# A half-swap of a matrix by memory-to-memory transfers: one walk over the rows replaced by eight

## The chip, the cores and the metric

The kernel runs on one core of one Trainium2 chip. Its time is the device time of the program in microseconds. It was run twice before the change: 822.33 us and 824.99 us, median 823.66 us.

## The reference

The input `x` is a matrix of 8192 x 8192 float32 numbers, 268.44 MB.

```python
def reference(x: np.ndarray) -> np.ndarray:
    return np.fft.ifftshift(x)
```

On an even-sized matrix this swaps the halves of both axes: output row `r` is input row `r + 4096` (modulo 8192), and in each row the left 4096 columns and the right 4096 columns change places. No number is changed. A row is 32 KiB long and half a row is 16 KiB, so everything the kernel does is to move 16384 runs of 16 KiB each from one place in the device memory to another.

## The kernel before, in words

There is no arithmetic and nothing is staged on chip. Two instruction streams, SyncE (SP, `nc.sync`) and ScalarE (ACT, `nc.scalar`), issue transfers that go straight from `x` to `out`, both of them in device memory. The core has 16 DMA engines, and the transfers of both queues run on the same 16.

`copy` (lines 26 to 32) issues one transfer: 256 rows of one half, 4 MiB. Its access pattern has three levels (line 28): 16 rows that lie next to each other, then 16 steps of `step * C` elements, then the 4096 elements of half a row. With `step = ENGINES = 16`, the outermost level counts neighbouring rows and the middle one jumps 16 rows ahead. The outermost level is the one that can be dealt out to the 16 engines. An engine that has index `k` of it moves rows `k`, `k + 16`, `k + 32` and so on, so that at one time the 16 engines are at 16 neighbouring rows, 32 KiB apart. The source address is that of row `row + 4096` and of the opposite half.

The loop (lines 36 to 39) takes 1024 rows at a time, which is four blocks of 256. For each block SP gets the left half of the output (`h = 0`), and ACT the right half (`h = hc`) of the block two further on, modulo four, so 512 rows away. Over the whole kernel SP writes the left half of `out` and ACT the right half, with 32 transfers each. The order of work is written out by hand; nothing but the two queues and the semaphores at which each transfer reports decides what runs when. The framework gives the transfers eight semaphores in turn, four to a queue, so that the fifth transfer of a queue is issued when the first one of that queue has landed.

Of the kernel before, what the change touches and what calls it, by code (L numbers as in the profile page):

```python
# [1 line left out]

# [4 lines left out]


ENGINES = 16


@with_exitstack
def kernel(
    ctx: ExitStack,
    tc: tile.TileContext,
    x: bass.AP,
    out: bass.AP,
):
    nc = tc.nc
    R, C = x.shape  # L20
    hr = R // 2
    hc = C // 2
    per = 16
    rows = ENGINES * per

    def copy(queue, row, h, step):

        dims = [[C, ENGINES], [step * C, per], [1, hc]]
        queue.dma_start(
            out=bass.AP(out.tensor, out.offset + row * C + h, dims),  # L30
            in_=bass.AP(x.tensor, x.offset + (row + hr) % R * C + hc - h, dims),
        )

    for first in range(0, R, 4 * rows):
        for n in range(4):
            copy(nc.sync, first + n * rows, 0, ENGINES)
            copy(nc.scalar, first + (n + 2) % 4 * rows, hc, ENGINES)


# [1 line left out]
_INS = ['x']  # L43
_OUTS = [((8192, 8192), 'float32')]


def kernel(**inputs):
    import numpy as _np
    import concourse.bacc as _bacc
    import concourse.tile as _tile  # L50
    from concourse import mybir as _mybir
    from concourse.bass_utils import run_bass_kernel_spmd as _run

    nc = _bacc.Bacc("TRN2", target_bir_lowering=False, num_devices=1)  # L54
    arrays, args = {}, []
    for name in _INS:
        a = _np.ascontiguousarray(inputs[name])
        if a.dtype.kind in "iu":
            a = a.astype(_np.int64)
        arrays[f"in_{name}_dram"] = a  # L60
        args.append(nc.dram_tensor(f"in_{name}_dram", a.shape, _mybir.dt.from_np(a.dtype), kind="ExternalInput").ap())
    for i, (shape, dtype) in enumerate(_OUTS):
        dt = _mybir.dt.from_np(_np.dtype(dtype))
        args.append(nc.dram_tensor(f"out_{i}_dram", shape, dt, kind="ExternalOutput").ap())
    with _tile.TileContext(nc) as tc:
        kernel(tc, *args)
    r = _run(nc, [arrays], core_ids=[0])
    got = tuple(r.results[0][f"out_{i}_dram"] for i in range(len(_OUTS)))
    return got[0]
```

## Time and profile before

| | |
|---|---|
| median of the two timed runs | 823.66 us |
| span of the profiled execution (first to last instruction) | 812.4 us |
| its own whole time | not given apart from the span |
| bytes read, bytes written | 268.44 MB, 268.44 MB |
| transfers | 32 on SP, 32 on ACT, 4096 KB each |
| duration of one issue (median) | 571 ns on SP, 578 ns on ACT |
| from issue to landing (median) | 101.0 us |

The profile of this kernel has hardly any compute in it: four small constants that GpSimd sets at the start. What there is to read are the rows on the DMA engines. "DMA" is the mean busy share of the 16 engines, "GB/s" is what they moved in one direction (every byte is read once and written once, so the memory sees twice that). A packet is one run of 16 KiB, or the short write by which an engine reports a finished transfer. Times in a table of windows count from the start of the span, and a packet is counted whole in the window in which it starts, so that the share of a short window can exceed 1.

### The profile page before, as it was taken

The numbers are of one execution on the slowest core, as the hardware profiler recorded it, in microseconds if no ns is written. First come the engines' busy times: TensorE is split into PE (matmuls) and PEld (weight loads), VectorE is DVE, ScalarE is ACT, GpSimd is POOL, SyncE is SP. The second block draws the span as 40 slices with busy tenths as digits, with TensorE's granted clock in tenths as the row PEclk, the third lists the DMA queues.
The fourth block names the chain that finished last, engine by engine and source line by source line (L and its number), as shares of the span: only waits on it lengthen the run. The fifth ranks groups of instructions, "written<-read, shape, count | busy, mean of one in ns | idle before, by whom it ended". The sixth has DMA issues, their size and how long they took to land. (4 is left out here: it accounts for less than half of the span.)

```text
span 812.4 us, 109 instructions
## 1 busy us (share of the span) xinstructions
POOL 0.2 (0%) x4
## 2 busy tenths in 40 slices
POOL 0000000000000000000000000000000000000000
DMA  9999999999999999999999999999999999999998
GB/s 307 331 331 336 335 331 331 335 325 337 334 332 336 331 333 332 334 339 332 332 334 331 329 331 334 332 328 333 330 334 335 334 328 333 332 331 330 338 331 280
DMA packets 17408, 268.44 MB, mean 330 GB/s; under 512 B 1024, under 2 KB 1024, under 8 KB 1024
## 3 DMA queue, kind: packets, MB, share of 16 engines
q1 hardware_dynamic: 8704, 134.22, 49.7%
q10 hardware_dynamic: 8704, 134.22, 49.5%
HBM read 268.44 MB, written 268.44 MB: 661 GB/s over the span
## 5 line engine op out<-in xcount | busy, mean ns | idle before, releaser
L54 POOL MEMSET const-bfloat16-1.0<- 128x1 bf16 x1 | 0.1, 101 | 0.0
L54 POOL MEMSET const-uint8-127<- 128x1 uint8 x1 | 0.1, 101 | 0.0
L54 POOL MEMSET const-float32-0.0<- 128x1 f32 x1 | 0.1, 98 | 0.2 <-issue 0.2
L54 POOL MEMSET const-float32-1.0<- 128x1 f32 x1 | 0.1, 98 | 0.0
## 6 DMA issues: line engine op xcount, KB each, us to landing
out_dram<-in_x_dram SPq DMA_DIRECT2D x32, 4096.0 KB, 101.0
out_dram<-in_x_dram ACTq DMA_DIRECT2D x32, 4096.0 KB, 101.0
```

The costliest lines, as they stand in the source:

```text
L54: nc = _bacc.Bacc("TRN2", target_bir_lowering=False, num_devices=1)
```

## The change

The loop is replaced by eight walks of 1024 rows each, one after the other, that cover the 8192 rows. All of them make `copy` transfers of another form, and each differs from the others in the order of the halves, in the distance between the rows of the two queues, or in both.

```diff
-    per = 16
-    rows = ENGINES * per
+    block = 256
+    part = 4 * block
-    def copy(queue, row, h, step):
-
-        dims = [[C, ENGINES], [step * C, per], [1, hc]]
+    def copy(queue, row, order, rows=block):
+        h = order[0] * hc
+        dst = out.offset + row * C + h
+        src = x.offset + (row + hr) % R * C + hc - h
+        to, of = [[C, rows]], [[C, rows]]
+        if len(order) == 2:
+            step = (order[1] - order[0]) * hc
+            to, of = to + [[step, 2]], of + [[-step, 2]]
         queue.dma_start(
-            out=bass.AP(out.tensor, out.offset + row * C + h, dims),
-            in_=bass.AP(x.tensor, x.offset + (row + hr) % R * C + hc - h, dims),
+            out=bass.AP(out.tensor, dst, to + [[1, hc]]),
+            in_=bass.AP(x.tensor, src, of + [[1, hc]]),
         )
+    def walk(first, sync, scalar):
+        for a, b in zip(sync, scalar):
+            copy(nc.sync, first + a[0] * block, a[1])
+            copy(nc.scalar, first + b[0] * block, b[1])
+    def whole(blocks, order):
+        return [(b, order) for b in blocks]
+    def halves(blocks, order):
+        return [(b, (h,)) for b in blocks for h in order]
+    def near(first):
+        for row in range(first, first + part // 2, ENGINES):
+            copy(nc.sync, row, (1, 0), ENGINES)
+            copy(nc.scalar, row + part // 2, (1, 0), ENGINES)
-    for first in range(0, R, 4 * rows):
-        for n in range(4):
-            copy(nc.sync, first + n * rows, 0, ENGINES)
-            copy(nc.scalar, first + (n + 2) % 4 * rows, hc, ENGINES)
+    left = [(b, (0,)) for b in (0, 1, 2, 3)]
+    right = [(b, (1,)) for b in (2, 3, 0, 1)]
+    for n, (sync, scalar) in enumerate((
+        (left, right),
+        (whole((0, 2), (1, 0)), whole((1, 3), (1, 0))),
+        (whole((0, 1), (1, 0)), whole((2, 3), (1, 0))),
+        (whole((0, 2), (0, 1)), whole((1, 3), (0, 1))),
+        (halves((0, 2), (0, 1)), halves((1, 3), (0, 1))),
+        (halves((0, 1), (0, 1)), halves((2, 3), (0, 1))),
+        (whole((0, 2), (1, 0)), whole((1, 3), (0, 1))),
+        (None, None),
+    )):
+        if sync is None:
+            near(n * part)
+        else:
+            walk(n * part, sync, scalar)
```

In words, with the walks numbered 0 to 7:

- Walk 0 has the same blocks, halves and queues as before (SP left halves, ACT right halves 512 rows away). Only the pattern is another: its outermost level counts 256 rows.
- Walks 1, 2, 3 and 6 move whole rows, 256 at a time (8 MiB), both halves of a row in turn: the pattern is 256 rows, 2 halves, 4096 elements. Walk 1 takes the right half of the output first and has the queues 256 rows apart; walk 2 does the same 512 rows apart; walk 3 is walk 1 with the left half first; in walk 6 SP takes the right half first and ACT the left half first, 256 rows apart.
- Walks 4 and 5 move one half of 256 rows in one transfer and then the other half in the next, left first on both queues; the queues are 256 rows apart in walk 4 and 512 in walk 5.
- Walk 7 (`near`) moves whole rows, right half first, but in transfers of 16 rows (512 KiB), 32 of them per queue, with the queues 512 rows apart.

Where the outermost level has 256 rows and an engine takes 16 successive ones, the 16 engines are 16 rows or 512 KiB apart at one time. In walk 7, as before the change, they are at neighbouring rows. The built program has per queue, in this order: 4 transfers of one half; 4 of whole rows; 2 of whole rows; 8 of one half; 2 of whole rows; 32 small ones: 52 in place of 32. The runs stay 16 KiB long, and there are 16384 of them as before.

## The prediction

> **What bounds the kernel now.** I read the page from the top. Compute is nothing, so the first rows that matter are those on the DMA engines, in forty slices of 20.3 us, and the totals by queue.
>
> ```profile
> span 812.4 us, 109 instructions
> DMA  9999999999999999999999999999999999999998
> GB/s 307 331 331 336 335 331 331 335 325 337 334 332 336 331 333 332 334 339 332 332 334 331 329 331 334 332 328 333 330 334 335 334 328 333 332 331 330 338 331 280
> DMA packets 17408, 268.44 MB, mean 330 GB/s; under 512 B 1024, under 2 KB 1024, under 8 KB 1024
> q1 hardware_dynamic: 8704, 134.22, 49.7%
> q10 hardware_dynamic: 8704, 134.22, 49.5%
> HBM read 268.44 MB, written 268.44 MB: 661 GB/s over the span
> ```
>
> The 16 DMA engines carry packets for 99.2% of the span (49.7% + 49.5%), half of it for each queue, and the rate lies between 325 and 339 GB/s in every slice but the first and the last. So the time is packets times the time of one: 17408 packets less 1024 short reports are 16384 runs of 16 KiB, 1024 to an engine, and 0.992 x 812.4 / 1024 is 787 ns each. Only a change of that 787 ns can move the time much.
>
> Next come the issues of line 29, and what SP waits for.
>
> ```profile
> L29 SPq DMA_DIRECT2D out_dram<-in_x_dram x32: 571/571/652, 0.7 to 708.6; - x32
> L29 ACTq DMA_DIRECT2D out_dram<-in_x_dram x32: 578/578/881, 0.7 to 713.5; - x32
> DMA to landing us min/median/max: 25.6/101.0/103.4
> ```
>
> ```profile
> SPq L29 <- DMA out_dram<-in_x_dram: 689.4, 28, 25.3
> ```
>
> An issue takes 0.57 us; 28 of SP's 32 wait for a transfer to land (24.6 us each), and a transfer lands 101.0 us after its issue, four periods of 25.3. Each queue is four transfers ahead. The issue side is idle 97% of the time.
>
> Last, is 787 ns a fixed cost? The table of windows shows the beginning and the end (columns: window, length, GpSimd busy, clock, DMA share, GB/s).
>
> ```profile
> 2.20:3.20 1.00, 0.00 (x0) 1.00 0.97 262
> 3.20:5.20 2.00, 0.00 (x0) 1.00 1.09 426
> 5.20:7.20 2.00, 0.00 (x0) 1.00 0.90 328
> 7.20:9.20 2.00, 0.00 (x0) 1.00 1.08 377
> 9.20:13.20 4.00, 0.00 (x0) 1.00 1.00 319
> ...
> 808.00:810.00 2.00, 0.00 (x0) 1.00 0.54 180
> 810.00:812.40 2.40, 0.00 (x0) 1.00 0.02 7
> ```
>
> The first packet starts about 2.2 us into the span. From 2.2 to 9.2 us the mean is (262 + 2 x 426 + 2 x 328 + 2 x 377) / 7 = 361 GB/s, and from then on it is 319 to 339. In the first 3 us only SP's queue has packets, and the 16 engines began together; the trace's packets of that time last 611 to 690 ns after a first set of about 1000, and 611 ns is also about the shortest of the whole run. So an engine can carry a packet in 611 ns, and in the steady state it takes 787: the memory behind all 16 holds them back. The last packets end within some 2 us of each other, so the engines keep step to the end.
>
> **The sum to start from.** 268.44 MB at the steady 332 GB/s is 808.6 us. The other 15.1 us of the 823.66 us median are 3.8 us of the span (its start, the uneven end) and 11.3 us around the span; the change touches none of them. One walk of 1024 rows is 33.55 MB, 101.1 us.
>
> **The change part by part.**
>
> *Bytes and packets.* The runs stay 16 KiB and 16384 in number: 0 us. Transfers rise from 64 to 104, so reports from 1024 to 1664; in the trace a report occupies its engine for 9 ns, so 640 / 16 x 9 ns = 0.4 us, added.
>
> *Issues, walks 0 to 6.* 20 issues per queue of 4 or 8 MiB. One of 512 rows of runs may take as long as two of 571 ns, 1.1 us. What hides it is the four transfers already queued, 101 us or more: 0 us; with no cover it would be 20 x 1.1 = 22 us. At a joint of two walks nothing waits, since the queues run on.
>
> *Issues, walk 7.* 32 issues of 512 KiB on each queue, one per 3.2 us if the rate holds (33.55 MB / 332 / 32). The issue takes 0.57 us of it. The four-deep lead shrinks to 4 x 2 x 0.524 MB = 4.2 MB, or 12.6 us of work. A slot comes back when the slowest engine has reported: about 2 us of unevenness (the end rows), 0.57 us of issue, 1.5 us from issue to first packet (0.7 to 2.2 us), some 4 us in all. Hidden: 0 us. Without the lead, each of the 32 rounds would cost up to 4 us, 128 us; I take 0, since 12.6 is three times 4.
>
> *The order of addresses, seven walks.* Before, 16 engines are at 16 neighbouring rows. In walks 0 to 6 they are 512 KiB apart (if an engine takes 16 successive rows of the 256), and in walks 1, 2, 3, 6 and 7 an engine does both halves of a row in turn. No row of this trace has such a spacing. The nearest ones are the rates that the same traffic takes by chance in short stretches, here in forty slices of 5 us:
>
> ```profile
> GB/s 331 324 338 334 351 315 315 338 344 331 341 321 351 334 324 344 288 357 331 347 324 321 354 315 347 315 334 360 334 328 341 328 341 338 341 321 331 338 324 344
> ```
>
> Five of forty are at 315 or less and five at 351 or more; I take these as the ends. Seven walks are 234.9 MB: 707.5 us at 332, 745.7 at 315 (+38), 669.2 at 351 (-38). I take 332, so 0. The reason is that the 20 us slices don't vary though queue, blocks and addresses do: each engine gets its sixteenth of a shared rate, and the same rate holds in the slices where one queue happens to have most of the packets as where they are even. That is how a limit on the sum of reads and writes looks, 661 GB/s, and the sum is not changed.
>
> Here the Trainium skill has a rule against the change. "DMA: Bandwidth & Descriptors", in "Latency and other measured facts", gives copies of 16 KiB pieces between memory tensors less rate at large power-of-two row pitches: 207 GB/s at 512 KiB against 214 unhampered, 164 at 2 MiB. By it the seven walks would take 214 / 207 x 707.5, 24 us more, an estimate of 848 us in all. No trace of this case has that pitch between engines yet.
>
> *Walk 7's addresses* are near ones, as now: 0 us; in turn or not, the same ends would be -5 and +5 us.
>
> Sum: 823.7 + 0.4 = 824 us.
>
> **The rivals.**
>
> *Slower: the engines collide.* Sixteen streams that stand 512 KiB apart and move in step hit the same parts of the memory at once more often than sixteen neighbouring rows do. For it: the engines do keep step, and the packets already lose 787 - 611 = 176 ns to something shared. Against it: with two queues an engine is rarely at the same point of its row as the next. At 315 GB/s in seven walks the time is 862 us. It decides from a rate of 324 in the seven walks, which is 725.0 us, 17 us more. If pairs of engines serialised outright, it could go far beyond; 288 GB/s, the lowest slice, would give 815.6 for the seven walks, 932 us. This is also where the Trainium skill's pitch rule ends.
>
> *Faster: the order matters and neighbouring halves help.* [...] For it: 361 GB/s in the first 7 us shows that the memory can give more to a more orderly pattern. Against it: that lasted 7 us of 809. At 361 in the five walks in turn (167.8 MB), these take 464.8 in place of 505.4 us, 783 us in all. It decides from 344 GB/s in these five, 17.6 us less. The Trainium skill's "HBM Reference", "Specifications (TRN2)", states about 716 GB/s for the memory of a pair of cores; the sum of 661 is 92% of it, and at 716 this kernel would take an estimated 750 + 15 = 765 us, so it leaves little room below.
>
> *The change doesn't do what it says.* If the 16 engines are dealt the rows of a 256-row transfer one by one, walk 0 is the kernel before, and only the order of halves changes elsewhere. Nothing in the trace says how rows are dealt. The time would be 824, so I count it with the forecast.
>
> *Walk 7 runs dry.* If a slot came back in 16 us and not 4, walk 7 would take 32 x 4 = 128 us in place of 101, 851 us in all. For it: only 512 KiB per transfer. Against it: the 4 us above.
>
> **How the numbers follow.** Forecast, no change of rate (or walks that cancel): 0.45, 824 us, own range 808 to 840. Engines collide: 0.31, around 862. Walk 7 dry: 0.04, 851. Neighbouring halves help: 0.20, around 783. A measurement of this kernel can tell some 2% from no change. Chances: faster 0.20, same 0.45, slower 0.35. The range of 8 in 10 leaves out the lower half of the fast case and the far end of the slow one: 788 to 875 us.
>
> **What would show it.** The eight walks come one after the other, so windows of about 101 us of the new profile price each by its GB/s: 325 to 339 in all eight would bear the forecast out. Below 324 in walks 0 to 6 with about 332 in walk 7 is the collision, and walk 0 alone is its clean test, since it differs from the kernel before only in the spacing. Above 344 in walks 1, 2, 3, 6 and 7 and not in 0, 4, 5 is the gain from neighbouring halves. A DMA share well below 1 in walk 7 is a queue run dry. What would make the forecast wrong is that the 787 ns depend on which addresses are in flight together, and not only on their sum.

## The result, and the profile after

The changed kernel takes 846.22 us (846.17 and 846.28), the kernel before 823.66 us: 1.029 times as long, 95% interval 1.022 to 1.035. That is slower, inside the range of 788 to 875 us, but not the likeliest case of the forecast, which was 824 us.

The page of the kernel after: the span, the rates in forty slices of 21.1 us, and the totals.

```profile
span 844.4 us, 149 instructions
DMA  9999999999999999999999999999999999999998
GB/s 301 331 322 317 331 308 315 303 317 303 310 319 307 313 311 310 315 311 309 314 326 331 323 335 326 332 328 330 331 326 310 313 316 314 304 321 329 331 328 294
HBM read 268.44 MB, written 268.44 MB: 636 GB/s over the span
```

The engines carry packets all the time, as before. The row that was flat (325 to 339) now has steps: four slices of 317 to 331 after the start, fifteen near 311, ten near 328, five near 311 again, and 321 to 331 at the end. Windows laid inside the eight walks give one number to each (columns: window, length, GpSimd busy, clock, DMA share, GB/s).

```profile
2.00:102.00 100.00, 0.00 (x0) 1.00 1.00 327
104.00:210.00 106.00, 0.00 (x0) 1.00 1.00 309
212.00:318.00 106.00, 0.00 (x0) 1.00 1.00 311
321.00:425.00 104.00, 0.00 (x0) 1.00 1.00 312
428.00:527.00 99.00, 0.00 (x0) 1.00 1.00 330
530.00:628.00 98.00, 0.00 (x0) 1.00 1.00 330
631.00:736.00 105.00, 0.00 (x0) 1.00 1.00 311
739.00:838.00 99.00, 0.00 (x0) 1.00 1.00 326
```

The DMA share is 1.00 in every walk, so no walk starves; the packets themselves take longer. Four walks are slow, 1, 2, 3 and 6, and these are the four that move both halves of a row in turn with the engines 16 rows apart. The three with halves apart (0, 4, 5) are not slow, though they were written for the same spacing (E1 below asks whether they have it), and neither is walk 7, in turn at neighbouring rows. Which half comes first (1 against 3), whether the queues are 256 or 512 rows apart (1 against 2) and whether they have like or opposite halves (1 against 6) makes 2 to 3 GB/s.

Four walks of 33.55 MB at 311 in place of the 329 that E1 below has on the same stretch of runs are 134.2 / 0.311 - 134.2 / 0.329 = 23.6 us; the measured difference is 22.6.

The waits of SP and the landing of the small transfers answer to the rows of issue shown before:

```profile
SPq L39 <- DMA out_dram<-in_x_dram: 607.6, 48, 53.6
```

```profile
out_dram<-in_x_dram SPq DMA_DIRECT2D x32, 512.0 KB, 12.8
```

48 of 52 issues wait for a landing, so SP is still four transfers ahead throughout, and a small transfer lands 12.8 us after its issue, four periods of 3.2.

### The profile page after: what moved, and what is told of

Its sections match the earlier page's. It is cut to its first block, busy times and chain, and to the rows that moved or that the text cites. A ratio compares the mean times of both kernels' runs of the same rounds, so it can differ in the third digit from the quotient of the medians.

```text
span 844.4 us, 149 instructions
## 1 busy us (share of the span) xinstructions
POOL 0.2 (0%) x4
## 6 DMA issues: line engine op xcount, KB each, us to landing
out_dram<-in_x_dram SPq DMA_DIRECT2D x32, 512.0 KB, 12.8
out_dram<-in_x_dram ACTq DMA_DIRECT2D x32, 512.0 KB, 12.8
```

## The experiments

Two notes for the numbers. The kernel before took 822.3 us beside E1 to E8 (run on chips 5 and 1) and 813.6 us beside E9 to E12 (chips 0 and 14), so rates of E9 to E12 are some 1% above those of the others and ratios are taken within a group. And most kernels here are surveys like the changed kernel itself: eight walks of 1024 rows, each read from a window of its own.

The first theory, A: the loss needs far engines and halves in turn together, because the runs in flight then lie at few different places of the memory, and collide there. Rivals: B, the large three-level transfer of whole rows is slow as a form; C, the spacing alone costs; D, halves in turn cost by themselves.

**E1, walk 0 in all eight places.**

```diff
-    for n, (sync, scalar) in enumerate((
-        ...
+    for n in range(8):
+        walk(n * part, left, right)
```

> All eight walks as walk 0: halves apart, queues in opposite halves, engines 512 KiB apart. Against the kernel before it changes the spacing of the engines alone. Theory A (the loss needs both, far engines and halves in turn, because then the runs in flight lie at few different places within the 512 KiB that an engine walks): 327 to 331 GB/s in every walk, the profiled span within 1.5% of that of the kernel before. Rival C (far spacing alone costs): walk 0 of the changed kernel had 327 GB/s where the kernel before had 334, so 2% slower in every walk.

Measured: 821.93 us against 822.27, ratio 0.9997 (0.9971 to 1.0023). Two of its walks:

```profile
412.00:508.00 96.00, 0.00 (x0) 1.00 1.00 331
514.00:610.00 96.00, 0.00 (x0) 1.00 1.00 326
```

All eight have 326 to 331, so this form of transfer costs nothing. What looked like 327 against 334 was the difference between two groups of runs.

That would end C if the engines of these walks really stood 512 KiB apart, which is not shown. In the trace, the issue of such a transfer is recorded as `dst_num_elem=[256,1]`, the inner count first, so with a count of 1 in the outer place. Every other form here has 16 or more in it: the kernel before `[16,16]`, walk 1 `[2,256]`, walk 3 `[1,512]`. If the engines are dealt the 256 rows one by one, they stand at neighbouring rows, as in the kernel before, and walk 0 has no new spacing. The times of the packets speak for that. Take a queue's packets in order of start, in sets of sixteen. In the kernel before, sets 0 to 3 and 8 to 11 of each 256 rows (rows 0 to 63 of each 128) took 825 ns a packet and the other sets 748. Averaged over walks and queues, the two groups of sets differ by 71 ns in walk 0 of the changed kernel and by 82 ns in walks 4 and 5 (there the other sets are the slow ones), but only by 21 ns in walks 1, 2, 3 and 6. E1 has 49 ns.

**E2, walk 1 in all eight places.**

```diff
+    for n in range(8):
+        walk(n * part, whole((0, 2), (1, 0)), whole((1, 3), (1, 0)))
```

> All eight walks as walk 1: whole rows in turn, right half first, queues 256 rows apart, 8 MiB transfers, engines 512 KiB apart. If the loss belongs to that form and not to the place of the walk in the kernel or in memory, every eighth has 309 to 312 GB/s and the time is 865 to 875 us, 2 to 3% above the changed kernel. If it came from the joints between unlike walks, it would be near 824 us.

Measured: 862.00 us, ratio 1.050 (1.045 to 1.054), 312 to 316 GB/s in every walk, about 3 us under what was expected. Walk 1:

```profile
112.00:214.00 102.00, 0.00 (x0) 1.00 1.00 312
```

The loss belongs to the form of the walk, not to its place in the kernel or to the joints.

**E3, form or place.** All in turn or nearly; transfers of 16 rows, one per engine, have the same small size as walk 7's.

```diff
+    def small_far(first, off=0):
+        for b in (0, 2):
+            for j in range(ENGINES):
+                r = first + b * block
+                copy(nc.sync, r + j, [("r", 16, ENGINES), ("h", -1, 2)], 1)
+                copy(nc.scalar, r + block + (j + off) % 16, [("r", 16, ENGINES), ("h", -1, 2)], 1)
```

> Eight walks of 1024 rows, queues 256 rows apart unless said. 0: in turn, 256-row transfers, as walk 1. 1: the same rows in the same order, but in transfers of 16 rows, one per engine, 512 KiB apart. 2: in turn, 16 neighbouring rows, as walk 7. 3, 4, 5, 7: halves change after every 2, 4, 8, 16 rows of an engine. 6: as 1, with ACT half a run (8 rows) away within each engine's 16 rows. Theory A (few places within the 512 KiB in flight at once): 0 and 1 near 311 GB/s, 2 near 326, 3 to 7 rising from 311 to 330 with the number of rows, and 6 above 1, about 325, since the queues then lie at different places. Rival B (the large three-level transfer of whole rows is what is slow): 0 near 311, 1 and 6 near 326 as 2 is, and 3, 4, 5, 7 all near 330. Rival D (both halves of a row one after the other by one engine cost by themselves, wherever the others are): 0, 1, 6 near 311, 3 to 7 at 330 at once.

| walk | GB/s |
|---|---|
| 0, in turn, 256 rows per transfer | 314 |
| 1, in turn, 16 rows per transfer, engines 16 rows apart | 310 |
| 2, in turn, 16 rows per transfer, neighbouring rows | 328 |
| 3, 4, 5, halves change after 2, 4, 8 rows | 314, 314, 311 |
| 6, as 1, ACT 8 rows off | 323 |
| 7, halves change after 16 rows (recorded as `[256,1]`, as in E1) | 329 |

Walk 1 is slow in transfers of 512 KiB, as slow as walk 0 in transfers of 8 MiB: B falls. (Walks 1 and 2 differ in the stride of one level and in the distance of the queues, 256 and 512 rows; E4 has both strides at 512 rows and the same difference.) Walk 6 shows that the place of one queue against the other counts. D fails on walks 3 to 5, and A's own rise over them did not come either: there is a jump between 8 and 16 rows. It falls where the recorded form changes, from `[8,16]`, which names the 16 places of the engines 16 rows apart, to `[256,1]`.

**E4, the spacing in turn.**

```diff
+    def turn(first, n):
+        for r in range(first, first + part // 2, 16 * n):
+            both(r, r + part // 2, [("r", 1, 16 * n), ("h", -1, 2)], 1)
```

> All walks but the last are in turn, queues 512 rows apart; the engines stand 1, 2, 4, 8, 16, 32 rows apart in walks 0 to 5 (transfers of 0.5 to 16 MiB), and 17 and then 15 rows apart in walk 6; walk 7 is halves apart at 16 rows. Theory A (few places within a power-of-two stretch in flight at once): 326 GB/s at 1, falling with the distance to 311 at 16 and as low or lower at 32; 17 and 15 bring it back to 325 to 331, since successive engines then stand at different places; walk 7 at 330. Rival B (the large transfer of whole rows): 1 and 2 near 326, the rest near 311, and 17 and 15 near 311 as well. Rival D (in turn by itself): all but the first near 311.

The walks at 8, 16 and 32 rows, the one at 17 and 15 rows, and the one with halves apart:

```profile
309.00:406.00 97.00, 0.00 (x0) 1.00 1.00 330
411.00:513.00 102.00, 0.00 (x0) 1.00 1.00 310
520.00:645.00 125.00, 0.00 (x0) 1.00 1.00 252
652.00:754.00 102.00, 0.00 (x0) 1.00 1.00 307
762.00:852.00 90.00, 0.00 (x0) 1.00 1.00 327
```

At 1, 2, 4 and 8 rows it is 328 to 330; the fall sets in between 8 and 16 rows (256 and 512 KiB), and 32 rows cost almost a quarter of the rate. An even fall from 1 on, as A had it, did not come. B and D, which had the rest near 311, fail at 4 and 8 rows. The odd spacing did not help, which is a miss of theory A as it stood. In these walks the rate follows the rows per transfer, so here each engine does take a run of successive rows; dealt one by one, all six would be the same.

**E5, one part undone: 8 rows in place of 16 in walks 1, 2, 3 and 6.**

```diff
-        (whole((0, 2), (1, 0)), whole((1, 3), (1, 0))),
-        ...
+    def eight(first, a, b, order):
+        for n in range(4):
+            copy(nc.sync, first + a[n] * part // 8, order[0], part // 8)
+            copy(nc.scalar, first + b[n] * part // 8, order[1], part // 8)
```

> The changed kernel with one edit: in walks 1, 2, 3 and 6 the transfers have 128 rows in place of 256, so that the engines stand 8 rows (256 KiB) apart and not 16; halves, their order and the distance of the queues stay. Theory A (the engines' spacing in turn is what costs): those four walks go from 309 to 312 up to 330 GB/s, and the time from 846 down to 820 to 824 us. Rival D (halves in turn cost by themselves): still about 845 us.

Measured: 823.73 us, ratio to the kernel before 1.002 (0.9997 to 1.004). Walks 1 and 2 are now

```profile
106.00:204.00 98.00, 0.00 (x0) 1.00 1.00 326
208.00:306.00 98.00, 0.00 (x0) 1.00 1.00 329
```

Halving the transfers of those four walks, and with them the distance between engines, brings the ratio from 1.029 to 1.002, with halves still in turn, in the same order, on the same queues. The smaller size by itself is not the reason: in E3, transfers of 512 KiB with the engines 16 rows apart are as slow as those of 8 MiB.

**E6, how far apart the two queues are within a run.** E3's `small_far` with eight offsets of ACT.

```diff
+    for n, off in enumerate((0, 1, 2, 4, 6, 8, 10, 12)):
+        turn(n * part, off)
```

> All walks in turn, engines 16 rows apart, 16 rows per transfer, queues 256 rows apart plus an offset: when SP's engines are at row j of their runs of 16, ACT's are at row j + 0, 1, 2, 4, 6, 8, 10, 12 (modulo 16) in walks 0 to 7. Theory A2 (what counts is whether the runs in flight lie in unlike 256 KiB groups of 8 rows): the two queues are in unlike groups for offset/8 of the time up to 8 and (16 - offset)/8 beyond; from 311 GB/s at 0 to 323 at 8 that gives 311, 312.5, 314, 317, 320, 323, 320, 317. Rival A1 (any unlike row will do, as it spreads them over all places): 311 at 0 and some 320 or more at once from 2 on. Rival E (the offset does nothing; 323 was chance): 311 in all.

```profile
2.00:107.00 105.00, 0.00 (x0) 1.00 1.00 309
110.00:214.00 104.00, 0.00 (x0) 1.00 1.00 310
219.00:321.00 102.00, 0.00 (x0) 1.00 1.00 312
326.00:427.00 101.00, 0.00 (x0) 1.00 1.00 318
432.00:530.00 98.00, 0.00 (x0) 1.00 1.00 323
536.00:633.00 97.00, 0.00 (x0) 1.00 1.00 327
639.00:737.00 98.00, 0.00 (x0) 1.00 1.00 324
743.00:840.00 97.00, 0.00 (x0) 1.00 1.00 319
```

In the reports of this run the transfers of the two queues land on average 0.3 us apart, a tenth of the time of a row, so the offset is the distance. The rate climbs evenly to 8 rows and comes back as evenly: 4 and 12 give 318 and 319, 6 and 10 give 323 and 324. That is the shape of A2, with a rise of 18 GB/s where 12 was expected: with an offset of d rows out of 16, the queues are in unlike 256 KiB groups for d / 8 of the time up to 8, and for (16 - d) / 8 beyond. From 309 to 327 nearly the whole loss is undone by moving ACT a quarter of a MiB. A1, any unlike row, and E, chance, fall.

**E7, halves apart: spacing, and queues that run even.**

```diff
+                copy(nc.sync, a + j, [("r", 16, ENGINES), ("r", 1, 2)], 0)
+                copy(nc.scalar, b + (j + off) % 16, [("r", 16, ENGINES), ("r", 1, 2)], 1)
```

> Halves apart, SP left and ACT right halves, queues 512 rows apart as in walk 0 (0 rows in walk 4). Walks 0 to 4: engines 4, 8, 16, 32, 64 rows apart. Walks 5 to 7: 16 rows apart, in transfers of 2 rows per engine, so that the queues run even, with ACT 0, 4 and 8 rows away within each run of 16. Theory A: 330 at 4, 8, 16, and then falling, below 311 at 32 and below 253 at 64, as fewer places are left; walk 5 falls to about 311, since large transfers were saved only by ACT being some 3 rows behind, and walk 7 is back at 323 to 330. Rival D (only halves in turn cost): 327 to 330 in all eight.

The walk at 64 rows in large transfers, and the three in transfers of 2 rows:

```profile
413.00:511.00 98.00, 0.00 (x0) 1.00 0.99 328
516.00:616.00 100.00, 0.00 (x0) 1.00 1.00 312
622.00:720.00 98.00, 0.00 (x0) 1.00 1.00 326
725.00:822.00 97.00, 0.00 (x0) 1.00 1.00 322
```

At 4, 8, 16, 32 and 64 rows large transfers of halves apart keep 326 to 329: the expected fall at 32 and 64 did not come. All five are recorded with an outer count of 1, so by the rival of E1 none of them has the spacing that it was written for. Walks 5 to 7 name it in a level of its own (`[2,16]`), and walk 5 shows that halves apart can lose as much as halves in turn. So D falls for good, A's condition of halves in turn falls with it, and C, the spacing alone, stands again wherever the queues run even. By the reports ACT was one transfer, 2 rows, ahead in these three walks, so the queues were 2, 6 and 10 rows apart in place of 0, 4 and 8; E6 has 312, 323 and 324 at these distances, and here it is 312, 326 and 322.

**E8, a search for a better walk**, with neighbouring rows at six distances of the queues, and in turn at 8 rows.

```diff
+    for n, off in enumerate((512, 512 + 64, 512 + 128, 512 + 192, 512 + 256, 64)):
+        near(n * part, off)
+    turn8(6 * part, 0)
+    turn8(7 * part, 4)
```

> A search for a walk that beats both kernels. Walks 0 to 5: halves apart, engines at neighbouring rows as before the change, in transfers of 64 rows, with the queues 512, 576, 640, 704, 768 and 64 rows apart. Walks 6 and 7: in turn, engines 8 rows apart, 16 rows per transfer, ACT 0 and 4 rows away within each run of 8. In the kernel before, the packets in rows 0 to 63 of each 128 took some 820 ns and the others some 745, on both queues; if what collides is the like places of the two queues, 576 and 704 give 335 to 345 GB/s and 512, 640, 768 give 331. If 331 is a limit of the memory, all eight have 325 to 334.

All eight have 325 to 330 GB/s and the kernel takes 824.95 us. None of these eight orders is better than the kernel before, though the packets of that kernel take 825 ns in one half of the rows and 748 in the other.

**E9, the same at 32 rows**, where the loss is largest.

```diff
+    turn(1 * part, 0)
+    turn(2 * part, 4)
+    turn(3 * part, 8)
+    turn(4 * part, 16)
+    apart(5 * part, 0)
+    apart(6 * part, 8)
+    apart(7 * part, 16)
```

> Engines 32 rows (1 MiB) apart in all walks, queues 512 rows apart plus an offset. Walk 0: in turn in one transfer of 512 rows per queue. Walks 1 to 4: in turn in transfers of 16 rows, so that the queues run even, ACT 0, 4, 8, 16 rows away within each run of 32. Walks 5 to 7: halves apart in opposite halves, transfers of 2 rows per engine, ACT 0, 8, 16 rows away. Theory A2 (like places of the two queues collide, the fewer places the spacing leaves the worse): about 240 to 253 in walks 0, 1; rising over walks 2 and 3; walk 5 low as well, near 250, and walks 6 and 7 clearly above it. Rival D (halves in turn cost, halves apart don't): 253 in walks 0 to 4, 327 to 329 in walks 5 to 7.

Walks 1, 2, 3, and then 5 and 6:

```profile
130.00:254.00 124.00, 0.00 (x0) 1.00 1.00 259
260.00:368.00 108.00, 0.00 (x0) 1.00 1.00 293
374.00:474.00 100.00, 0.00 (x0) 1.00 1.00 318
...
586.00:704.00 118.00, 0.00 (x0) 1.00 1.00 271
710.00:809.00 99.00, 0.00 (x0) 1.00 1.00 319
```

8 rows between the queues are worth 59 GB/s in turn and 48 with halves apart. Here the expectation that halves apart would be low with even queues came true, though the low walks lie above what was expected of them: 265 and 259 in walks 0 and 1 (240 to 253), 271 in walk 5 (near 250). The same form as walk 0 had 252 in E4. (ACT was one transfer ahead, so the distances are 1, 5, 9 and 2, 10 rows.) 16 rows give 315, no more than 8.

**E10, one queue alone.**

```diff
+    turn(0 * part, 16)
+    apart(1 * part, 16)
+    near(2 * part)
+    turn(3 * part, 8)
+    turn(4 * part, 32)
+    apart(5 * part, 32)
+    turn(6 * part, 4)
+    turn(7 * part, 16)
```

> All transfers on SP, ACT idle. Walks: 0 and 7 in turn at 16 rows, 1 apart at 16, 2 apart at neighbouring rows, 3 in turn at 8, 4 in turn at 32, 5 apart at 32, 6 in turn at 4. If it is the two queues that collide with each other, in turn at 16 and 32 rows is as fast as the others here, 325 to 334 in all. If it is the engines among themselves, 0 and 7 have 300 to 312 and 4 some 250 or less, and 1 and 5 are slow too, since a single queue has no second place to go to. In the first 3 us of the kernel before, one queue alone moved packets in 611 to 690 ns; if a single queue as such is faster, some walk is above 340.

Walks 0, 3, 4 and 5:

```profile
2.00:105.00 103.00, 0.00 (x0) 1.00 1.00 321
...
314.00:411.00 97.00, 0.00 (x0) 1.00 1.00 333
416.00:532.00 116.00, 0.00 (x0) 1.00 1.00 277
536.00:632.00 96.00, 0.00 (x0) 1.00 1.00 332
```

Measured: in turn 333 at 4 and 8 rows, 321 and 318 at 16, 277 at 32; halves apart 326 at 16 and 332 at 32 (both recorded with an outer count of 1), neighbouring rows 327. So the second queue is the smaller part of it: with one queue, 32 rows in turn still cost a sixth, where two queues lost almost a quarter in E4. The engines of one queue lose among themselves too. Neither of the two expectations holds in full. One queue alone does not exceed 333 here either.

**E11, ACT 8 rows off in a whole kernel**: E6's walk 5 in all places.

```diff
+    for n in range(8):
+        turn(n * part, 8)
```

> All eight walks in turn with engines 16 rows apart and 16 rows per transfer, queues 256 rows apart, and ACT 8 rows away within each run of 16. In single walks this had 323 and 327 GB/s. Theory A2: 268.44 MB at 327 GB/s is 821 us, so with start and end 825 to 835 us, against 862 us where all walks are in turn without the offset. Rival E (the gain of a walk doesn't hold over a kernel): 850 us or more.

Measured: 816.12 us against 813.61, ratio 1.004 (1.0025 to 1.006), 330 to 333 GB/s in each walk. Expected were 825 to 835, from rates of E3 and E6, whose group ran 1% below this one. E2, the same walk with ACT not moved and in larger transfers, has the ratio 1.050: the offset takes nine tenths of the loss away with engines 512 KiB apart and halves in turn.

**E12, the best walk of E10 as a kernel**, all on SP, 8 rows apart, 128 rows per transfer.

```diff
+    for r in range(0, R, 128):
+        copy(nc.sync, r, [("r", 1, 128), ("h", -1, 2)], 1)
```

> All rows on SP alone, in turn, right half first, 128 rows per transfer, engines 8 rows apart: the walk that had the highest rate with one queue, 334 GB/s against 326 for neighbouring rows beside it in the same kernel. If that is a property of the walk, 268.44 MB take 804 us, some 0.3 to 1% less than the kernel before on the same chip. If all walks without collisions end at the same limit of the memory, it is within 0.5% of it on either side.

Measured: 814.38 us against 813.55, ratio 1.0011 (0.9999 to 1.0023): the same, with half the queues. No version timed here beats the kernel before.

## Why the prediction was right and wrong

**What bounds the kernel**: right. The DMA engines are full in every walk, and all of the difference lies in the time of a packet.

**The sum to start from**: a term mis-sized. 11.3 us around the span was the span of one execution against the median of others; in the runs since it is 1.8 to 2.2 us (846.17 against 844.4, 822.29 against 820.5). With that, the profiled execution took about 814 us, like the runs beside E9 to E12. So 332 GB/s was not the rate of a run of 823.66 us; 329 was, and part of what the windows seem to show is that.

**Issues and reports**: right. 0 us, even with 50.5 us for the longest issue, where two at 0.57 had been allowed: six issues on each queue, of large transfers or of ones queued behind them, took 15 to 50 us, and the lead of four transfers covered it.

**Walk 7**: right. 326 GB/s, DMA share 1.00, landing after 12.8 us where 12.6 had been worked out.

**The order of addresses, "I take 332, so 0"**: the step that failed. Its reason was that a flat rate shows a limit on the sum of reads and writes. A ceiling exists (no walk of E1 to E12 exceeds 334), but no run shows that it lies on the sum of reads and writes, and a pattern can fall below it: the kernel before and four of the eight walks are at it, and the other four moved 311 in place of 329, 23.6 us. That the rate before did not vary with addresses was so only in slices of 20 us: in its packets the rows 0 to 63 of each 128 took 825 ns and the others 748, changing over every 6.3 us.

**The rival "engines collide"**: right that engines 512 KiB apart lose and in its sign; that they hit the same parts of the memory is not shown. It was wrong in its place. It had all seven walks at 315, and named walk 0 as the clean test. Walk 0 has no loss at all (E1, 0.9997), but by its packets it probably never had the spacing. The loss is in four walks and larger in each, 311, which is why 846 lies between 824 and 862; that it fell inside the range is owed to the range holding both. All walks in turn took 862 (E2).

The rule that the Trainium skill gives ("DMA: Bandwidth & Descriptors", "Latency and other measured facts") led to an estimate of 848 us, close to 846. The trace agrees with its direction and with its total by accident: three of the seven walks lose nothing (and probably do not have the pitch), four lose 5.5% where the rule has 3.3%.

**The rival "the change doesn't do what it says"**: probably right for walks 0, 4 and 5 (E1), which the prediction counted with the forecast, and wrong for walks 1, 2, 3 and 6, where the loss follows the spacing (E4, E5).

**The rival "neighbouring halves help"**: wrong, the walks in turn are those that lose here, and at 8 rows or at neighbouring ones in turn is the same as halves apart (E5, E8). Its 361 GB/s in the first 7 us was read too high: a packet counts whole in the window in which it starts, and by the share of each packet inside the window it is 350.

**What is shown and what stays open.** Shown: the loss needs a spacing of 16 rows or more (E4, E5); in small transfers with the spacing named it goes with how often the two queues are in like 256 KiB groups of their runs (E6, E9, E11); halves in turn are not necessary for it (E3 walks 3 to 5, E7 walk 5, E9 walk 5).

Argued, not shown: that what collides are parts of the memory chosen by address bits, in the reads or in the writes. In favour is that 8 rows between the queues undo what 1 and 2 rows hardly touch, and that the loss deepens from 16 to 32 rows.

Argued, not shown: that large transfers of halves apart escape because their engines stand at neighbouring rows. In favour are the times of the packets (E1; in walks 5 to 7 of E7, halves apart with the spacing named, the same two groups of sets differ by 27 ns) and that every walk recorded with an outer count of 1 kept 325 to 332 GB/s whatever spacing it was written for (E1, E3 walk 7, E4 walk 7, E7 walks 0 to 4, E10 walks 1 and 5). Two other reasons do not fit. One is that ACT runs 3 rows behind in E1 (its transfers land 4.8 us after SP's): in E4 walk 7 it is one row ahead, and the rate is 327, where E6 has 310 at one row. The other is that the engines of one queue keep closer step in turn: the sixteen reports of a transfer spread over 0.5 to 1.6 us in E2 and over 0.9 to 3.3 in E1, but over 2.8 to 4.1 in E7 walk 5, which loses, and alike in walks 4 and 5 of E10, of which one loses. No run moves large transfers of one half with the places of the engines named 16 rows apart; the nearest is E3 walk 5, with 8 rows per engine, and it had 311. That the odd spacing of E4 fails because the queues still stood at like places is not tested either.

## What to carry to other kernels

A flat rate on full DMA engines says that one pattern of addresses is at a ceiling, not that any pattern would be; when the order of a copy is changed, bound it by a run of the new pattern, one walk per window of a single kernel. If engines must stand half a MiB or more apart, set the second queue's place off by a quarter of a MiB, or split the transfer so that the engines stand at 256 KiB or less. Before a walk is used as the test of a spacing, look at the counts that its transfer is recorded with, and at whether its packets show it. Compare a span only with the time of its own execution.

## What the runs showed of the hardware

- Where nothing was lost, copies from memory to memory ended at 325 to 333 GB/s each way with one queue or two, with transfers from 0.5 to 16 MiB (E7, E8, E10, E11).
- In turn, the rate by the distance of the engines was 328 to 330 GB/s up to 256 KiB, 310 at 512 KiB and 252 at 1 MiB (E4; 265 for the last in E9).
- 256 KiB between the two queues raised it from 309 to 327 at 512 KiB (E6), and from 259 to 318 at 1 MiB (E9).
- With one queue alone, in turn, it was 333 GB/s at 128 and 256 KiB, 318 to 321 at 512 KiB and 277 at 1 MiB (E10).
- The issue of a transfer of 8 MiB took up to 50.5 us, and it cost nothing (DMA share 1.00 in every walk).
